# Prompt attention of a hybrid decoder layer: transposing and splitting a head's probabilities one turn ahead of its value products

## The chip, the cores and the metric

The kernel runs on one core of a Trainium2 chip. The metric is the device time of one execution in microseconds. The core's engines run their own instruction queues in order and wait for one another by semaphores: TensorE (PE in the profile; its weight loads are PEld), VectorE (DVE), ScalarE (ACT), GpSimd (POOL) and SyncE (SP), which here only issues DMAs.

## The reference

One layer of a decoder serves 512 prompt tokens and 8 x 4 sample tokens with shared weights: a gated feed-forward, a mixer of four recurrent (HGRN2) and four latent-attention (MLA) heads, an output projection, and a second feed-forward. Each part has norms before and after it. The change lies in the causal softmax attention of the four MLA heads over the 512 prompt tokens:

```python
s = (jnp.einsum('bqhr,bsr->bhqs', ql, c_kv) + jnp.einsum('bqhd,bsd->bhqs', qr, k_rope)).astype(jnp.float32) * scale
s = jnp.where(k_pos[None, None, None, :] <= qp[None, None, :, None], s, -jnp.inf)
p = jax.nn.softmax(s, axis=-1).astype(c_kv.dtype)
return jnp.einsum('bqhs,bsr->bqhr', p, c_kv)
```

The result is projected per head (`w_uv`), concatenated with the recurrent heads and multiplied by `w_out`. The kernel uses the unabsorbed form: per-head keys and values are made first, so that a head's output is its probabilities times its values.

## The kernel before, in words

Nearly all products are made in three passes of a reduced-precision fp32 type: an operand is split into a high part (a cast on ACT, line 170) and a remainder (a subtraction on DVE, line 171), and high x high, high x low and low x high are accumulated in PSUM. Weights arrive by DMA into `wraw` and are split the same way, by a cast on ACT (`wh`, L250) and a subtraction on DVE (`wl`, L251).

The stages in time: first feed-forward (to about 380 us), recurrent heads (to about 575), latent keys and values, then the prompt attention (about 628 to 698 us), into which the output projection of the first 256 tokens (`project(0)`) is woven; after it the decode attention of the sample tokens and the second feed-forward of the first 256 tokens, interleaved; then the rest.

The prompt attention goes through eight turns: four heads for the first 256 tokens (x = 0), then the same heads for the next 256 (x = 1). A turn's work for one head and half is:

- `soft` (L1202 to L1215): per block of 128 query rows (two per turn, qt), the scores on PE into a PSUM bank `s`, then maximum on DVE, exponential on ACT, reciprocal and scaling on DVE. The probabilities are in `pe`. In turns 0 to 3 a block is 128 or 256 keys wide, in turns 4 to 7 384 or 512.
- `value`, which first transposes `pe` on PE in pieces of 128 x 128 into a PSUM bank `tp` (L1225), splits each bank into `PTh` (ACT, L170) and `PTl` (DVE, L171), and then makes the products with the values into a bank `o` (L1234), six of them in turns 0 to 3 and twelve in turns 4 to 7. ACT copies `o` out (L1236).

`soft` runs two turns ahead of `value` (LOOK = 2). Around them stand in each turn: the query projection of a later head (`prep`, L259 with `acc<-q`, turns 0 and 1), the split of a query half (`qsplit_n`), the latent query of the sample tokens (`latent`, L1184 and L1185, turns 0 to 3), and from turn 4 the output projection (`acc<-uha` under L259; its columns are copied by L784 and squared into the norm's sum `ssp` by L298 and L300). The first half of the projection's inputs, the recurrent heads, is there early, so its first column is also begun early. After the last column the sum is made by L191, the norm's factor `s_post` by L197 and L198, and DVE multiplies and adds (L312, L313) to make the inputs `uha` (L207) and `ula` (L208) of the second feed-forward, whose products are L277.

Between these stand small pieces of the decode attention: copies of `qsT` (L1243 on ACT, L1245 on DVE), and the scores of the new tokens (L1317 and L1318 on PE, their maximum L1320 on DVE).

The order on each engine is not the order of the text. A scheduler places the instructions by their place in the text (earlier is more urgent) and by its own estimate of when their inputs are ready. PSUM has eight banks: four for `acc`, and four that `s`, `tp`, `o`, `qa` and `pr` take in a fixed cycle of tags, `CYC = ("ps", "po", "ps", "pm")`, where ps has two banks and po and pm one each. A tile that takes a bank waits until the reader of the tile before it is done. `pe` has three buffers (PEB), `PTh` and `PTl` two (PTB).

Of the kernel before, what the change touches and what calls it, by code (L numbers as in the profile page):

```python
# [110 lines left out]
def hybrid_step_kernel(  # L111
# [18 lines left out]
    def mk(shape, dt, tag, bufs=1, pool=None):  # L130
        return (pool or cur[-1]).tile(shape, dt, name=tag, tag=tag, bufs=bufs)
# [10 lines left out]
    def ps(name, tag="ps", own=False):  # L142
        if tag == "ps" and not own:
            tag = CYC[turns[0] % 4]
            turns[0] += 1
        return pp.tile([P, 512], F32, name=name, tag=tag, bufs=NPS[tag])

    def f32(ap):
        return ap.bitcast(F32)
# [19 lines left out]
    def split(hi, lo, src, eng=None):  # L169
        nc.scalar.copy(hi, src)  # L170
        (eng or nc.vector).tensor_tensor(lo, src, f32(hi), op=ALU.subtract)  # L171
# [121 lines left out]
    def wcols(w, k0, kt, c0):  # L293
        return w[c0 // P, :, k0 : k0 + kt]
# [494 lines left out]
    with scope("mix") as mx_:  # L789
# [5 lines left out]
        q0 = mk([P, 2, KQ, W2], F32R, "q0", pool=dK)  # L795
# [287 lines left out]
        with scope("at2"):  # L1083
# [83 lines left out]
            def prep(hd):  # L1167
                w = weight([w_q[hd]], KQ)
                a = [gemm(w, Q[x]) for x in BOTH]
                qn = mk([P, HS[0]], F32, "qn", QNB)  # L1170
                g = W2 - HS[0]
                nc.vector.tensor_tensor(qn, a[0][:, : HS[0]], s_q[0][:, : HS[0]], op=ALU.mult)
                nc.vector.tensor_tensor(qnb[:, hd, :g], a[0][:, HS[0] :], s_q[0][:, HS[0] :], op=ALU.mult)
                nc.vector.tensor_tensor(qnb[:, hd, g:], a[1], s_q[1], op=ALU.mult)
                qsplit_n(hd, 0, qn)

            def qsplit_n(hd, x, qn):
                qq[hd, x] = [mk([P, 2 * P], F32R, n, 2) for n in ("qnh", "qnl")]
                split(*qq[hd, x], qn[:, : 2 * P])
# [35 lines left out]
                    nc.vector.tensor_scalar_mul(pe[:, :N], pe[:, :N], sm)  # L1215
                return pes

            def value(hd, x, pes):
                q0 = 2 * x
                PTh = mk([P, 4, 2 * P], F32R, "PTh", PTB)  # L1220
                PTl = mk([P, 4, 2 * P], F32R, "PTl", PTB)
                for qt in (q0, q0 + 1):
                    tp = ps("tp")
                    for k in range(qt + 1):
                        nc.tensor.transpose(tp[:, k * P : (k + 1) * P], pes[qt][:, k * P : (k + 1) * P], ident)  # L1225
                    ds = slice((qt - q0) * P, (qt - q0 + 1) * P)
                    split(PTh[:, : qt + 1, ds], PTl[:, : qt + 1, ds], tp.rearrange("p (k t) -> p k t", k=4)[:, : qt + 1])
                o = ps("o")
                n = 0
                hs = slice(hd * P, (hd + 1) * P)  # L1230
                for k in range(q0 + 2):
                    lo = P if k == q0 + 1 else 0
                    for a_, b_ in ((Vh, PTh), (Vh, PTl), (Vl, PTh)):
                        nc.tensor.matmul(o[:, lo : 2 * P], a_[:, k, hs], b_[:, k, lo:], start=n == 0, stop=n == 3 * q0 + 5, skip_group_check=True)  # L1234
                        n += 1
                nc.scalar.copy(oT[x][:, NH + hd, : 2 * P], o[:, : 2 * P])  # L1236
# [21 lines left out]
            heads = [(hd, x) for x in BOTH for hd in range(NH)]  # L1258
            for hd in range(LOOK):
                prep(hd)  # L1260
            pe_ = [soft(*heads[i]) for i in range(LOOK)]
            pj = None
            for i, (hd, x) in enumerate(heads):
                if i + LOOK < len(heads):
                    if i + LOOK < NH:
                        prep(i + LOOK)
                    else:
                        qsplit_n(i + LOOK - NH, 1, qnb[:, i + LOOK - NH])
                    pe_.append(soft(*heads[i + LOOK]))
                if i < NH:  # L1270
                    latent(i)
                if i == PJ0:
                    pj = project(0, to_ffn)
                    next(pj)
                value(hd, x, pe_[i])
                if i == NH - 1:
                    dq = mk([P, 2, KQ * HS[1]], F32, "q1", pool=dK)
                    qbd = [dq[:, 0, k * 320 : (k + 1) * 320].rearrange("p (j q) -> p j q", j=10) for k in range(2)]
                    qrep = dq[:, 1, : 10 * P].rearrange("p (j q) -> p j q", j=10)
                    nc.gpsimd.memset(dq[:, 0, :640], 0.0)  # L1280
                if i == DP:
                    decode_prep()
                    qsplit(0)
                for _ in range(PJ[i]):
                    next(pj, None)
                if i in W1:
                    w0.append(weight([wcols((w_g, w_u)[W1.index(i)][1], 0, KD, 0)], KD))
# [422 lines left out]
```

## Time and profile before

| what | value |
|---|---|
| median of 3 runs | 1250.35 us (1250.27 to 1250.57) |
| the profiled execution, its own time | 1243.16 us |
| its span, first to last instruction | 1241.4 us |
| mean granted TensorE clock | 0.999 |
| PE, DVE, ACT, POOL busy | 98%, 79%, 60%, 6% of the span |
| transposes of the probabilities (L1225) | 40, from 636.5 to 694.5 us |
| casts and subtractions of `tp` into PTh and PTl | 16 and 16, from 636.9 to 696.3 us |

A row of the profile in order of time gives start, duration, engine, line, operation, output and inputs, their shapes and the count of merged instructions; in brackets stands how long the engine was idle before it and what ended the idle time. Durations overlap: products of 256 columns follow each other every 0.12 us though each lasts 0.28. The profiled execution is one execution, 7.19 us faster than the median of the runs, so sums are made against its own time and then carried over as differences.

### The profile page before, as it was taken

What the parts mean: (1) busy time and instruction counts of PE and PEld (TensorE: products, weight loads), DVE (VectorE), ACT (ScalarE), POOL (GpSimd) and SP (SyncE); (2) the same over time, 40 slices, a digit from 0 to 9 for tenths busy, and PEclk for the clock granted to TensorE, in tenths of its full rate; (3) what the DMA queues carried; (4) which work ended last, traced back from release to release, by engine and by line L of the source; (5) the groups of instructions that cost most, each with busy time, mean ns of one, the idle gap of its engine ahead of it and who ended that gap; (6) DMA issues with size and microseconds to landing.
All of it is one profiled execution on the core that took longest, in us unless ns stands there. A gap on an engine that the chain in (4) does not pass through costs nothing.

```text
span 1241.4 us, 29997 instructions
## 1 busy us (share of the span) xinstructions
PE 1215.0 (98%) x12366; PEld 1151.3 (93%) x12366; DVE 982.7 (79%) x1976; ACT 738.8 (60%) x1559; POOL 76.5 (6%) x80
## 2 busy tenths in 40 slices
PE   8999999999999999999999999999999999999997
PEld 6999999999999989988898888888888999999997
DVE  7897788878678888786877899999998778566665
ACT  7675545455366744545758766666656776554455
POOL 0000000000000000000001312322310000000000
PEclk9999999999999999999999999999999999999999
DMA  6232333232264213333233868878776635545451
GB/s 238 86 115 90 103 103 102 86 99 91 62 221 147 82 54 105 88 94 130 85 105 117 339 214 303 310 282 323 258 275 232 198 106 188 184 137 188 150 151 60
DMA packets 73113, 195.59 MB, mean 158 GB/s; under 512 B 12336, under 2 KB 27728, under 8 KB 68240
## 3 DMA queue, kind: packets, MB, share of 16 engines
q1 hardware_dynamic: 64512, 150.47, 37.3%
q0 software_dynamic: 7168, 41.95, 9.2%
q8 instruction: 97, 1.59, 0.5%
q10 hardware_dynamic: 1296, 1.26, 0.3%
q14 instruction: 40, 0.33, 0.1%
HBM read 183.97 MB, written 9.67 MB: 156 GB/s over the span
## 4 chain that ended last, share of the span: by engine, by line
PE 79%; DVE 11%; ACT 7%; issue 2%; DMA 2%; SPq 0%; DVEq 0%; ACTq 0%
PE acc L259 29%; PE acc L277 13%; PE dn L259 8%; PE Y L575 7%; PE X L575 4%; PE Z L575 4%; DVE kh L1381 3%; PE acc L731 3%; DVE wl L251 2%; ACT wh L250 1%; PE s L1393 1%; ACT pbuf L1417 1%; DMA wraw<-w_g 1%; PE pa L952 1%; PE o L1426 1%
## 5 line engine op out<-in xcount | busy, mean ns | idle before, releaser
L250 ACT CAST wh<-wraw 128x1024 fp32r<-128x1024 f32 (+2 forms) x194 | 185.0, 957 | 164.3 <-PE acc L259 103.7
L251 DVE TENSOR_TENSOR wl<-wraw,wh 128x1024 fp32r<-128x1024 f32 (+2 forms) x194 | 214.6, 1108 | 72.2 <-ACT wh L250 71.6
L277 PE MATMUL acc<-uha,wh 128*128 128x256 f32 (+1 forms) x528 | 155.5, 295 | 0.1
L277 PE MATMUL acc<-uha,wl 128*128 128x256 f32 (+1 forms) x528 | 150.0, 285 | 0.8 <-DVE wl L251 0.7
L277 PE MATMUL acc<-ula,wh 128*128 128x256 f32 (+1 forms) x528 | 150.5, 286 | 0.0
L259 PE MATMUL acc<-uhb,wh 128*128 128x288 f32 (+1 forms) x432 | 128.0, 296 | 0.0
L259 PE MATMUL acc<-uhb,wl 128*128 128x288 f32 (+1 forms) x432 | 127.0, 295 | 1.0 <-DVE wl L251 0.8
L259 PE MATMUL acc<-ulb,wh 128*128 128x288 f32 (+1 forms) x432 | 127.5, 295 | 0.0
L277 PEld LDWEIGHTS acc<-uha,wh 128*128 128x128 f32 x528 | 99.2, 188 | 8.8 <-issue 7.9
L277 PEld LDWEIGHTS acc<-uha,wl 128*128 128x128 f32 x528 | 99.2, 188 | 2.3 <-DVE wl L251 1.6
L277 PEld LDWEIGHTS acc<-ula,wh 128*128 128x128 f32 x528 | 99.4, 188 | 1.6 <-issue 1.2
L259 PEld LDWEIGHTS acc<-uhb,wl 128*128 128x128 f32 x432 | 81.2, 188 | 1.6 <-DVE wl L251 1.6
L259 PEld LDWEIGHTS acc<-uhb,wh 128*128 128x128 f32 x432 | 81.0, 187 | 0.2 <-ACT uhb L170 0.2
L259 PEld LDWEIGHTS acc<-ulb,wh 128*128 128x128 f32 x432 | 81.1, 188 | 0.1
L259 PE MATMUL dn<-hh,dh 128*128 128x272 f32 x256 | 74.3, 290 | 0.0
L259 PE MATMUL dn<-hh,dl 128*128 128x272 f32 x256 | 73.7, 288 | 0.0
L259 PE MATMUL dn<-hl,dh 128*128 128x272 f32 x256 | 73.6, 288 | 0.0
L277 PE MATMUL acc<-uhb,wh 128*128 128x272 f32 x176 | 52.8, 300 | 0.0
L1417 ACT COPY pbuf<-pt 32x64 f32<-32x64 f32 x192 | 46.5, 242 | 10.1 <-DVE pt L1413 7.3
L259 PE MATMUL acc<-hlb,wh 128*128 128x288 f32 x176 | 52.1, 298 | 0.0
L259 PE MATMUL acc<-hhb,wh 128*128 128x288 f32 x176 | 51.8, 298 | 0.0
L1393 PE MATMUL s<-kh,q 64*32 64x128 f32 x2560 | 48.0, 273 | 3.5 <-DVE kh L1381 3.5
(632 smaller groups left out, 3881.3 us busy)
## 6 DMA issues: line engine op xcount, KB each, us to landing
wraw<-w_u SPq DMA_DIRECT2D x66, 512.0 KB, 4.3
wraw<-w_g SPq DMA_DIRECT2D x65, 512.0 KB, 3.9
wraw<-w_d SPq DMA_DIRECT2D x40, 384.0 KB, 3.5
wraw<-w_in SPq DMA_DIRECT2D x24, 512.0 KB, 3.5
wraw<-w_d SPq DMA_DIRECT2D x32, 320.0 KB, 3.1
wraw<-w_d SPq DMA_DIRECT2D x16, 512.0 KB, 3.8
wraw<-w_o SPq DMA_DIRECT2D x16, 512.0 KB, 3.7
g_S<-state SPq DMA_DIRECT2D x4, 512.0 KB, 4.4
```

Source lines behind the costliest of these rows:

```text
L250: nc.scalar.copy(wh[:, :kt], w[:, :kt])
L251: nc.vector.tensor_tensor(wl[:, :kt], w[:, :kt], f32(wh[:, :kt]), op=ALU.subtract)
L259: nc.tensor.matmul(out, a, b, start=n == 0, stop=n == last)
L277: nc.tensor.matmul(acc[:, :n], a[:, k], b[:, k], start=k + i == 0, stop=k == kt - 1 and i == 2)
L575: nc.tensor.matmul(bank, a[p][:, k], b[q][:, k], start=first and k + n == 0, stop=k == 3 and n == 2, skip_group_check=True)
L731: nc.tensor.matmul(accs[x, d], wts[d][p][:, k], hs[k // 2][q][:, k % 2, x], start=k + n == 0, stop=k == nf - 1 and n == 2)
L952: nc.tensor.matmul(po[es, c].rearrange("p (n m) -> p n m", m=m), kx[:, cs], up(qx[:, cs], m), start=True, stop=True, skip_group_check=True)
L1381: nc.vector.transpose(kh[:, g].rearrange("p a j k -> p a (j k)"), src)
L1393: nc.tensor.matmul(self.s[r][c * 32 : c * 32 + 32, :P], q[rs, j], kh, start=st + jj == 0, stop=st == len(JS) - 1 and jj == 1, skip_group_c ...
L1417: (nc.scalar.copy if g else nc.vector.tensor_copy)(self.p[g * 32 : g * 32 + 32, c // 2, c % 2 * 4 : c % 2 * 4 + 4, self.i * 16 : self.i * ...
L1426: nc.tensor.matmul(o[g : g + 32, :R], self.p[:, c, a], self.craw[c][:, a], start=i + c == 0 and a < 4, stop=i + c == 2 and a >= 4, skip_gr ...
```

## The change

`value` is cut in two: `lay` transposes and splits, `value` makes the products. `lay` of turn 0 is called ahead of the loop, and in turn i `lay` of turn i + 1 is called ahead of `value` of turn i. No buffer count changes, and no instruction is added or removed.

```diff
-            def value(hd, x, pes):
+            def lay(x, pes):
                 q0 = 2 * x
                 PTh = mk([P, 4, 2 * P], F32R, "PTh", PTB)
                 PTl = mk([P, 4, 2 * P], F32R, "PTl", PTB)
...
                     ds = slice((qt - q0) * P, (qt - q0 + 1) * P)
                     split(PTh[:, : qt + 1, ds], PTl[:, : qt + 1, ds], tp.rearrange("p (k t) -> p k t", k=4)[:, : qt + 1])
+                return PTh, PTl
+
+            def value(hd, x, PTh, PTl):
+                q0 = 2 * x
                 o = ps("o")
                 n = 0
...
             pe_ = [soft(*heads[i]) for i in range(LOOK)]
             pj = None
+            pt_ = [lay(heads[0][1], pe_[0])]
             for i, (hd, x) in enumerate(heads):
...
                     next(pj)
-                value(hd, x, pe_[i])
+                if i + 1 < len(heads):
+                    pt_.append(lay(heads[i + 1][1], pe_[i + 1]))
+                value(hd, x, *pt_[i])
```

In the changed kernel the lines behind `lay` have higher numbers: the products are L1238, the copy of `o` L1240, the copies of `qsT` L1247 and L1249, the maximum of the new tokens' scores L1327.

The scheduler's order changes from the third query projection to the first steps of the decode attention, about 6% of PE's queue; before and behind it, and on SP and POOL throughout, it is the same. Three places follow. The first is PE behind the scores of turn 1 (`s<-causb,idb` is the last of them; `acc<-q` is the third query projection, q_4791 its split input).

```order
 L1204 LDWEIGHTS idb
 L1204 MATMUL s<-causb,idb 128x128
+L1225 MATMUL tp<-ident,pe 128x128
 L259 MATMUL acc<-q_4791,wh 128x272 x2
 L259 MATMUL acc<-q_4791,wl 128x272
+L1225 MATMUL tp<-ident,pe 128x128 x2
 L259 MATMUL acc<-q_4791,wh 128x272 x2
```

Turn 0's three transposes moved to here from behind turn 0's latent query, one projection later; turn 1's now stand there.

The second place is ACT in turns 3 and 4 (`ma<-o` is the copy of turn 3's output, `q<-qsT` the small copies of the decode attention, whose tile has another number in each kernel, the 512-wide exponential turn 5's and the 384-wide one turn 6's).

```order
-L170 CAST PTh<-tp 128x128
-L170 CAST PTh<-tp 128x2x128
-L1243 COPY q_8192<-qsT 32x128 x3
+L1247 COPY q_8207<-qsT 32x128
+L170 CAST PTh<-tp 128x3x128
+L1247 COPY q_8207<-qsT 32x128
+L170 CAST PTh<-tp 128x4x128
 L1213 ACTIVATE pe,sm<-s,mx 128x512
-L1243 COPY q_8192<-qsT 32x128 x6
+L1247 COPY q_8207<-qsT 32x128 x7
+L1240 COPY ma<-o 128x256
 L1213 ACTIVATE pe,sm<-s,mx 128x384
```

Turn 4's casts, 384 and 512 wide, took the place of turn 3's, 128 and 256 wide, and the copy of turn 3's output moved ahead of the 384-wide exponential, behind one small copy more. Further down in that queue the first of two weight casts (L250) moved behind five small copies.

The third place is DVE behind the projection's last column (L312, L313 and L208 make the inputs of the second feed-forward; the first two rows are turn 6's subtractions before, and turn 7's in the changed kernel).

```order
 L171 TENSOR_TENSOR PTl<-tp,PTh 128x3x128
 L171 TENSOR_TENSOR PTl<-tp,PTh 128x4x128
-L171 TENSOR_TENSOR PTl<-tp,PTh 128x3x128
+L1327 TENSOR_REDUCE mx<-s 128x1
+L1329 COPY q_8207<-mx 128x128
 L312 TENSOR_TENSOR ma<-ma,s_post 128x512 x2
-L313 TENSOR_TENSOR q_8227<-q_8227,ma 128x512 x2
-L171 TENSOR_TENSOR PTl<-tp,PTh 128x4x128
-L208 SCALAR_TENSOR_TENSOR ula<-q_8227,gv,uha 128x256 x4
+L313 TENSOR_TENSOR q_8242<-q_8242,ma 128x512 x2
 L312 TENSOR_TENSOR ma<-ma,s_post 128x512 x2
```

Turn 7's two subtractions left this stretch (they are now its first two rows), the maximum of the new tokens' scores moved ahead of the first L312, and the second pair of L312 ahead of the first `ula`.

## The prediction

> **What bounds the kernel now.** I read the profile's page first, then the windows of ten microseconds around the lines of the change, then the waits of TensorE (PE) between 620 and 760 us, and last the rows in order of time at each of those waits.
>
> ```profile
> PE 1215.0 (98%) x12366; PEld 1151.3 (93%) x12366; DVE 982.7 (79%) x1976; ACT 738.8 (60%) x1559; POOL 76.5 (6%) x80
> ```
>
> PE is busy 1215.0 of 1241.4 us, and the change neither adds nor removes an instruction. It can only fill or open gaps in PE's row, and 26.4 us of gap is all there is in the whole program. In a window row the columns are the stretch, its length, then the busy time of PE, PEld, DVE, ACT and POOL, the granted clock, the share of the DMA engines and GB/s.
>
> ```profile
> 650.00:660.00 10.00, 9.05 (x58) 7.08 (x57) 8.48 (x33) 8.53 (x28) 0.00 (x0) 1.00 0.00 0
> 660.00:670.00 10.00, 9.20 (x73) 8.74 (x73) 7.80 (x21) 9.65 (x26) 0.00 (x0) 1.00 0.16 54
> 690.00:700.00 10.00, 7.71 (x55) 6.76 (x56) 9.24 (x17) 8.00 (x20) 3.37 (x3) 1.00 0.62 238
> 700.00:710.00 10.00, 9.87 (x79) 9.44 (x78) 10.00 (x23) 5.59 (x14) 6.13 (x5) 1.00 0.96 354
> ```
>
> The prompt attention runs from about 628 to 698 us. PE's gaps are 0.95, 0.80 and 2.29 us in the first three rows, 4.0 us together. Two other engines are near full in places: ACT with 9.65 of 10 in 660 to 670, DVE with 9.24 and 10.00 from 690 on. The waits that made PE's gaps (engine, line, what it waited for: total, times, longest):
>
> ```profile
> PE o L1234 <- ACT PTh L170: 2.4, 2, 1.7
> PE tp L1225 <- ACT ma L1236: 1.0, 1, 1.0
> PE acc L259 <- DVE wl L251: 0.8, 1, 0.8
> PE tp L1225 <- ACT qsT L1185: 0.3, 1, 0.3
> ```
>
> Only the first row, 2.4 us, is value products waiting for the cast of their own transposes, which is what the change takes out of the way. It is 0.19% of the time. The second and fourth are transposes waiting for a PSUM bank that ACT still reads, the third is a weight of the projection.
>
> **The change part by part.** The 40 transposes (L1225), 16 casts (L170) and 16 subtractions (L171) of all eight heads stay; DMA issues and POOL keep their order. What moves is where they stand in PE's, ACT's and DVE's queues, and, since the scheduler writes the order anew, a few neighbours. I follow three places, called A, B and C, and name each head by its turn, 0 to 7.
>
> *A, turn 0 pulled in front of the third query projection.* Turn 0's transposes now follow directly behind the scores of turn 1. Here are PE's row at that place, DVE's two scalings that make turn 0's probabilities ready, and where the transposes stand before.
>
> ```profile
> 630.24 0.49 PE L259 MATMUL acc<-q,wh 128*128 128x272 f32 x2
> 630.88 0.29 DVE L1215 TENSOR_SCALAR pe<-pe,sm 128x128 f32<-128x128 f32 x1
> 631.47 0.35 DVE L1215 TENSOR_SCALAR pe<-pe,sm 128x256 f32<-128x256 f32 x1
> 636.53 0.31 PE L1225 MATMUL tp<-ident,pe 128*128 128x128 f32 x1
> ```
>
> Before, PE went on with the projection at 630.24 and came to the transposes at 636.53, long after the probabilities were there. Now the first transpose stands at 630.24 and its input is ready at 630.88 + 0.29 = 631.17: PE stops for 0.93 us, and the projection, whose inputs are there (it ran at 630.24), is queued behind it. The second pair needs 631.82; PE gets there at about 631.17 + 0.14 + 3 x 0.13 = 631.7, another 0.1 us. PE was full from 620 to 640 and the next waits of ACT and DVE there are for PE, so the loss is passed on. A = +1.0 us. Bounds: +0.4 if half of it comes back at the wait for qsT at 645.5 us (0.3) and the score wait after it, +1.1 if nothing does.
>
> *B, turns 1 to 5, 644 to 670 us.* The rows are those of the 1.0 us wait, of turn 4's last product, of ACT's two weight casts of the projection, and of PE's wait for the second of these.
>
> ```profile
> 657.27 1.83 ACT L1243 COPY q<-qsT 32x128 f32<-32x128 f32 x6
> 659.70 0.36 ACT L1236 COPY ma<-o 128x256 f32<-128x256 f32 x1
> 660.12 0.66 PE L1225 MATMUL tp<-ident,pe 128*128 128x128 f32 x4 [0.98 <-ACT ma L1236]
> 664.26 0.27 PE L1234 MATMUL o<-PTh,Vl 128*128 128x128 f32 x1
> 662.66 1.05 ACT L250 CAST wh<-wraw 128x1024 fp32r<-128x1024 f32 x1
> 667.85 1.05 ACT L250 CAST wh<-wraw 128x1024 fp32r<-128x1024 f32 x1
> 670.21 0.39 PE L259 MATMUL acc<-uha,wl 128*128 128x256 f32 x1 [0.76 <-DVE wl L251]
> ```
>
> The wait at 660.12 stays in kind: the transposes (now turn 5's) still stand behind turn 3's products, in the same bank, and ACT still runs its small copies (1.83 us, now seven) before it empties the bank. L1236 now stands ahead of the 384-wide exponential, so the wait ends some 0.4 us earlier, at about 659.7. Turn 4's twelve products follow with their casts done and PE is through with them near 661.7 instead of 664.26, with about 1.0 us more work behind it, counted in products. That lead has no taker: the projection's next weights come from ACT. Between 654 and 668 ACT now casts turns 4 and 5 instead of 3 and 4. By form the casts take:
>
> ```profile
> L170 ACT CAST PTh<-tp 128x512 fp32r<-128x512 f32 x4 | 2.4, 588 | 0.1
> L170 ACT CAST PTh<-tp 128x384 fp32r<-128x384 f32 x4 | 1.9, 478 | 0.4 <-PE tp L1225 0.4
> L170 ACT CAST PTh<-tp 128x256 fp32r<-128x256 f32 x4 | 1.5, 372 | 0.4 <-PE tp L1225 0.4
> L170 ACT CAST PTh<-tp 128x128 fp32r<-128x128 f32 x4 | 1.1, 267 | 0.0
> ```
>
> That is 588 + 478 - 372 - 267 = 427 ns more on an engine with 0.35 us to spare in ten, so the cast at 667.85 slides to about 668.3 and PE's restart at 670.21 to 670.6. The first weight (662.66) is also put behind five small copies, 5 x 0.3 = 1.5 us, and becomes a new wait of PE of about 0.8 us, paid out of the 1.0 us lead. B = +0.4 us. Bounds: -1.7 us if both waits (0.98 and 0.76) vanish, +1.0 us if the late first weight delays the second by its own 1.5 us less the 0.5 us that ACT could close up.
>
> *C, turns 6 and 7 at the end of the projection, 688 to 702 us.* Turn 6's transposes are done in turn 5; turn 7's take their place.
>
> ```profile
> 688.94 0.93 PE L1225 MATMUL tp<-ident,pe 128*128 128x128 f32 x7
> 691.57 0.39 PE L1234 MATMUL o<-PTh,Vh 128*128 128x256 f32 x1 [1.70 <-ACT PTh L170]
> 691.32 0.41 DVE L300 TENSOR_TENSOR ssp<-ssp,sq 128x256 f32<-128x256 f32 x1
> 691.88 0.67 PE L191 MATMUL pr<-ssp,ones 128*128 128x256 f32 x2
> 692.96 0.47 ACT L170 CAST PTh<-tp 128x384 fp32r<-128x384 f32 x1
> 693.94 1.28 DVE L312 TENSOR_TENSOR ma<-ma,s_post 128x512 f32<-128x512 f32 x2
> 695.49 0.39 PE L1234 MATMUL o<-PTh,Vh 128*128 128x256 f32 x1 [0.68 <-ACT PTh L170]
> 695.72 0.86 PE L1317 MATMUL s<-kss,qsT 128*128 128x32 f32 x6
> 696.34 0.68 DVE L171 TENSOR_TENSOR PTl<-tp,PTh 128x512 fp32r<-128x512 f32 x1
> 696.95 1.66 DVE L208 SCALAR_TENSOR_TENSOR ula<-q,gv,uha 128x256 fp32r<-128x256 f32 x4
> 698.42 0.33 PE L277 MATMUL acc<-ula,wh 128*128 128x256 f32 x1
> ```
>
> Both waits of 1.70 and 0.68 us go: turn 6's products run from about 689.4 to 690.9, turn 7's casts fall where turn 6's were. What is late next is the norm of the projection. Its sum (L191) needs ssp, which is ready at 691.32 + 0.41 = 691.73 in both kernels, so PE stands again from 690.9 to 691.8 and L191 moves only by 0.1 us. Then ACT is free of a cast (692.96) and has s_post some 0.4 us earlier. But DVE's queue now has the maximum of the new tokens' scores (L1320) ahead of L312, and these scores stand on PE behind L191 and one product of turn 7: 692.45 + 0.2 + 0.86 + 0.1 = 693.6, and with L1320 and L1322 L312 starts at 693.9 to 694.1, as before. Behind it four blocks of L312 now precede the first ula, where two and a PTl did: 694.0 + 6 x 0.6 = 697.6 against 696.95. PE, done with turn 7 at about 694.9, waits for the first ula until 697.6 + 0.4 = 698.0, against 698.42, and the second four ula come 0.6 us earlier, by the PTl that has left (696.34). C = -0.5 us. Bounds: -2.4 us if both waits vanish and no other comes, +0.7 us if PE needs the first ula 0.65 us later as DVE has it.
>
> From about 712 us every queue has its old order, and DVE is full (10.00 in 700 to 710), so a shift is passed on to the end. Sum: +1.0 + 0.4 - 0.5 = +0.9 us on the profiled execution, 1243.16 us (span 1241.4). The median of the runs shown lies 7.19 us above that execution; I add the difference to the median: 1250.35 + 0.9 = 1251.2 us, and call it no change, since a run of this kernel tells about 0.2%, 2.5 us, from nothing.
>
> **The rivals.**
>
> *The end of the projection gets longer and PE's clock falls back (slower).* In place C PE has a gap from 694.9 to 698.0 with two products in it. The start of the program shows what a pause can do:
>
> ```profile
> 5.36 1.12 PE L506 MATMUL pr<-xq,ones 128*32 128x272 f32 x4 [5.36 <-ACT xq L502]
> 7.48 0.43 PE L259 MATMUL acc<-xl,wh 128*128 128x272 f32 x1
> 7.71 0.43 PE L259 MATMUL acc<-xh,wl 128*128 128x272 f32 x1
> 9.62 0.29 PE L259 MATMUL acc<-xh,wh 128*128 128x272 f32 x1
> 9.75 0.33 PE L259 MATMUL acc<-xl,wh 128*128 128x272 f32 x1
> ```
>
> After 5.36 us of nothing, products start every 0.23 us, and from 9.62 every 0.13. Some 4.2 us at the slow step lose 4.2 x 0.10 / 0.23 = 1.8 us. After the gap of 1.70 us at 691.57 nothing of the kind shows, so the point lies between. If it is passed, and DVE's late ula costs its 0.7 us, the sum is 1.0 + 0.4 + 0.7 + 1.8 = 3.9 us: 1254.3 us. The Trainium skill (TensorE: Matmul & The Clock Gate, Part 1: The HAM clock gate) says that about 3.4 us without work halves the clock and as much work restores it; by it my gap is just too short and the sum stays as it is, while 0.5 us more would decide against the change. For it speaks that DVE decides this place; against it that the two products stand in the gap. 0.12.
>
> *The waits vanish and nothing takes their place (faster).* C gives its whole 2.4 us and B its 1.7 us against A's 1.0: 1250.35 - 3.1 = 1247.3 us. For it speaks that DVE loses 1.1 us of subtractions from its full stretch; against it that ssp, the bank and the weight casts are not touched by the change. 0.10.
>
> *The transposes were early enough anyway.* The two waits of the products in the table are those of turns 6 and 7; the turns before them show none, and A's loss, B's lead and C's gain cancel: 1250.4 us, give or take 0.5. 0.30.
>
> **How the numbers follow.** My forecast of 1251.2 us has 0.48. It and the third rival are no change, 0.78; slower by over 0.2% is the first rival and a little of the forecast's upper bound, 0.13; faster 0.09, most of the second rival. The bounds of the three terms add up to -3.7 and +2.8 us, but A is certain and B and C do not both reach their lower ends; with half of each rival's way the range is 1248.3 to 1253.6 us.
>
> **What would show it.** A: a wait of the first transpose for DVE's scaling of about 0.9 us near 630. B: a wait of transposes for L1236 near 660 of about the old length, and L250 rows later against turn 4's products. C: no product waiting for PTh, L1320 directly before L312, and a PE gap of 2 to 3 us before the first ula product. The forecast is wrong if A shows no wait, if L312 starts over 0.5 us earlier after L191 than before, or if products after the gap at C start every 0.23 us.

## The result, and the profile after

The changed kernel takes 1252.57 us (median of 22 runs, 1249.73 to 1254.25), the kernel before beside it 1250.17 us (22 runs). The ratio is 1.0014, with a 95% interval of 1.0007 to 1.002: about 1.75 us slower (0.9 to 2.5). That is no change by the bound of 0.2%, but not zero. It lies 1.4 us above the predicted 1251.2 us and inside the range.

The profiled execution of the changed kernel took 1252.31 us (span 1250.5 us). It can't be set beside the first profile of before as a whole: chips differ by 7 us in this kernel (two of those used run the kernel before in 1250.3 and 1250.6 us, one in 1243.6 us), and that profile took 1243.16 us. Of the 9.15 us between the two profiles some 6.5 arise behind 720 us. So positions below are counted from the first score of turn 0 (627.62 us before, 628.00 us in the changed kernel) and go to 712 us only; times are compared between kernels that ran on one chip.

First the waits of TensorE (PE) in the changed kernel, 620 to 760 us (total, times, longest):

```profile
PE acc L277 <- ACT uha L207: 1.5, 1, 1.5
PE acc L259 <- DVE wl L251: 1.4, 2, 0.8
PE s L1400 <- issue: 1.3, 3, 0.7
PE acc L277 <- DVE ula L208: 0.9, 1, 0.9
PE tp L1225 <- DVE pe L1215: 0.9, 1, 0.9
PE tp L1225 <- ACT ma L1240: 0.7, 1, 0.7
PE pr L191 <- DVE ssp L300: 0.6, 1, 0.6
```

The change did what it says: no product waits for a cast `PTh` any more, and the two waits of 1.70 and 0.68 us are gone. Five new ones stand in their place (1.54, 0.90, 0.88, 0.68 and 0.59 us); the bank's wait and one for a weight were there before. Up to the first ula product PE waited 4.4 us before (1.70 + 0.98 + 0.76 + 0.68 + 0.3 for qsT) and waits 6.4 us now (1.54 + 0.68 + 0.76 + 0.90 + 0.88 + 0.73 + 0.59 + 0.3).

The windows of ten microseconds around the three places:

```profile
650.00:660.00 10.00, 9.90 (x66) 8.04 (x66) 8.42 (x27) 8.16 (x25) 0.00 (x0) 1.00 0.02 8
660.00:670.00 10.00, 8.60 (x68) 7.73 (x68) 8.50 (x30) 9.69 (x28) 0.00 (x0) 1.00 0.04 7
690.00:700.00 10.00, 7.69 (x60) 6.92 (x58) 7.91 (x14) 7.64 (x18) 1.01 (x1) 1.00 0.92 366
700.00:710.00 10.00, 9.29 (x64) 9.25 (x65) 9.07 (x21) 5.86 (x17) 1.35 (x1) 0.83 0.95 336
```

In the last row the granted clock (third number from the end) is 0.83, and was 1.00 in the first profile of before. Cut finer, in the same columns:

```profile
697.00:700.90 3.90, 1.46 (x10) 1.06 (x10) 3.90 (x8) 3.36 (x8) 1.01 (x1) 1.00 0.83 270
700.95:704.30 3.35, 3.35 (x17) 3.35 (x17) 3.35 (x9) 2.24 (x7) 1.35 (x1) 0.50 0.84 339
704.40:710.00 5.60, 5.60 (x48) 5.56 (x48) 4.67 (x11) 2.57 (x8) 0.00 (x0) 1.00 0.96 334
```

For some 3.4 us TensorE has half its clock. The rows in order of time at that place:

```profile
694.52 0.67 PE L191 MATMUL pr<-ssp,ones 128*128 128x256 f32 x2 [0.59 <-DVE ssp L300]
696.20 0.19 DVE L1327 TENSOR_REDUCE mx<-s 128x1 f32<-128x32 f32 x1 [0.76 <-PE s L1325]
696.57 1.29 DVE L312 TENSOR_TENSOR ma<-ma,s_post 128x512 f32<-128x512 f32 x2
697.34 0.44 PE L1340 MATMUL b<-ident,q 128*128 128x128 f32 x2
697.81 1.05 ACT L250 CAST wh<-wraw 128x1024 fp32r<-128x1024 f32 x1
699.31 0.51 PE L277 MATMUL acc<-uha,wh 128*128 128x256 f32 x2 [1.54 <-ACT uha L207]
700.18 1.67 DVE L208 SCALAR_TENSOR_TENSOR ula<-q,gv,uha 128x256 fp32r<-128x256 f32 x4
700.72 0.43 PE L277 MATMUL acc<-ula,wh 128*128 128x256 f32 x1 [0.90 <-DVE ula L208]
700.94 0.41 PE L277 MATMUL acc<-uha,wl 128*128 128x256 f32 x1
701.15 0.41 PE L277 MATMUL acc<-uha,wh 128*128 128x256 f32 x1
...
704.35 0.28 PE L277 MATMUL acc<-ula,wh 128*128 128x256 f32 x1
704.47 0.28 PE L277 MATMUL acc<-uha,wl 128*128 128x256 f32 x1
```

PE is done with turn 7 and the small product behind it (L1340) at 697.78 and has only two products until 700.72. Then products start every 0.215 us, until 704.35, from where they start every 0.12. Between 700.72 and 704.35 there are some 17 of them: 17 x 0.095 = 1.6 us.

The wait at place A, with the two operations of VectorE (DVE) that end it and its sequel:

```profile
631.26 0.29 DVE L1215 TENSOR_SCALAR pe<-pe,sm 128x128 f32<-128x128 f32 x1
631.69 0.30 PE L1225 MATMUL tp<-ident,pe 128*128 128x128 f32 x1 [0.88 <-DVE pe L1215]
631.85 0.35 DVE L1215 TENSOR_SCALAR pe<-pe,sm 128x256 f32<-128x256 f32 x1
```

And the three at place B:

```profile
661.86 0.66 PE L1225 MATMUL tp<-ident,pe 128*128 128x128 f32 x4 [0.73 <-ACT ma L1240]
668.82 0.39 PE L259 MATMUL acc<-uha,wl 128*128 128x256 f32 x1 [0.68 <-DVE wl L251]
672.90 0.39 PE L259 MATMUL acc<-uha,wl 128*128 128x256 f32 x1 [0.76 <-DVE wl L251]
```

### The profile page after: what moved, and what is told of

The parts are those of the page before. It is cut to its first block, busy times and chain, and to the rows that moved or that the text cites. A ratio compares the mean times of both kernels' runs of the same rounds, so it can differ in the third digit from the quotient of the medians.

```text
span 1250.5 us, 29993 instructions
## 1 busy us (share of the span) xinstructions
PE 1221.5 (98%) x12366; PEld 1154.8 (92%) x12366; DVE 983.3 (79%) x1976; ACT 739.8 (59%) x1559; POOL 74.2 (6%) x80
## 4 chain that ended last, share of the span: by engine, by line
PE 86%; DVE 6%; ACT 5%; issue 1%; DMA 1%; DVEq 0%; SPq 0%; ACTq 0%
PE acc L259 30%; PE acc L277 17%; PE dn L259 8%; PE Y L575 7%; PE X L575 4%; PE Z L575 4%; PE s L1400 3%; PE acc L731 3%; PE o L1433 2%; ACT wh L250 1%; DVE wl L251 1%; DVE kh L1388 1%; PE pa L952 1%; PE acc L288 1%; PE zx L840 1%
## 5 line engine op out<-in xcount | busy, mean ns | idle before, releaser
L250 ACT CAST wh<-wraw 128x1024 fp32r<-128x1024 f32 (+2 forms) x194 | 184.9, 957 | 173.7 <-PE acc L259 107.6
L1400 PE MATMUL s<-kh,q 64*32 64x128 f32 x2560 | 52.0, 273 | 5.2 <-issue 3.4
```

The source lines that it names most:

```text
L250: nc.scalar.copy(wh[:, :kt], w[:, :kt])
L1400: nc.tensor.matmul(self.s[r][c * 32 : c * 32 + 32, :P], q[rs, j], kh, start=st + jj == 0, stop=st == len(JS) - 1 and jj == 1, skip_group_c ...
```

## The experiments

The theory to be tested: A and B are real losses that reach the end; at C the gap lets the clock fall, and that, too, reaches the end. The rivals: what is lost on PE is won back at later waits, or VectorE, which is full from 697 to 712 us, sets the pace, so that a slow TensorE costs nothing; or the clock has nothing to do with this gap.

All twelve in one table. The positions are differences of two rows of each profile: from turn 0's first score to the first ula product, to the sum L191 of `ssq` on PE (the next norm, some 80 products later), and to the first `kh` (the decode attention's first step on DVE). The last column is the stretch at half clock. A line "before, beside" gives the kernel before on the chip that ran the kernels below it.

| kernel | median, us | ratio to before beside it (95%) | ula | ssq | kh | half clock from, for |
|---|---|---|---|---|---|---|
| before (first profile) | 1250.17 | | 70.80 | 80.93 | 79.71 | none |
| changed | 1252.57 | 1.0014 (1.0007 to 1.0020) | 72.72 | 84.05 | 81.77 | 700.92, 3.41 |
| before, beside 1 to 4 | 1250.33 | | | | | |
| 1 changed again | 1252.58 | 1.0013 (1.0004 to 1.0022) | 72.72 | 84.13 | 81.82 | 700.44, 3.41 |
| 2 turn 0 not early | 1250.51 | 0.9995 (0.9986 to 1.0005) | 71.55 | 82.89 | 80.62 | 700.30, 3.41 |
| 3 gap filled | 1249.51 | 0.9997 (0.9987 to 1.0007) | 72.71 | 82.81 | 80.76 | none |
| 4 maximum behind | 1251.65 | 1.0005 (0.9996 to 1.0014) | 72.33 | 83.44 | 82.23 | 701.37, 3.41 |
| before, beside 5 to 8 | 1243.63 | | | | | |
| 5 before again | 1243.21, one run | | 71.85 | 81.45 | 80.24 | 691.58, 3.41 |
| 6 turns 6 and 7 only | 1243.84 | 0.9997 (0.9988 to 1.0006) | 71.08 | 83.18 | 80.92 | 697.15, 6.83 |
| 7 the same, filled | 1243.01 | 0.9994 (0.9985 to 1.0003) | 71.10 | 81.20 | 79.14 | none |
| 8 one us later | 1247.42 | 1.0022 (1.0013 to 1.0031) | 73.76 | 84.87 | 82.61 | 701.28, 3.41 |
| before, beside 9 to 12 | 1250.63 | | | | | |
| 9 changed, third time | 1252.01 | 1.0010 (1.0001 to 1.0019) | 72.71 | 84.05 | 81.79 | 701.17, 3.41 |
| 10 turn 0 not early, filled | 1248.82 | 0.9989 (0.9981 to 0.9998) | 71.50 | 81.58 | 79.53 | none |
| 11 as 7, again | 1247.50 | 0.9985 (0.9975 to 0.9996) | 71.10 | 81.19 | 79.14 | none |
| 12 as 11, maximum behind | 1247.31 | 0.9980 (0.9970 to 0.9989) | 70.72 | 80.58 | 79.37 | none |

### 1 and 9: the changed kernel again

No edit.

> The changed kernel once more, without any edit, as the measure for the three kernels that run beside it. Theory (the change costs time, about half of it because the clock falls after the gap at C): median near 1252.5 us, 1.0007 to 1.002 times the kernel before, with the granted clock at 0.83 or so between 700 and 710 us in most executions. Rival (the 1.75 us come from the chips or executions that the first comparison happened to meet): within 0.5 us of the kernel before, ratio interval around 1.0000.

> The changed kernel without an edit, as the measure for the three that run beside it on the same chip (chips were seen to differ by 7 us in the kernel before: 1250.3 and 1243.6 us). Theory: ratio to the kernel before 1.0007 to 1.002, as twice before; the granted clock at half for 3.41 us near 700 us. Rival (the loss belongs to the chip of the first two comparisons): ratio within 0.9995 to 1.0005 if this is the faster chip.

Measured: 1.0013 and 1.0010 times the kernel before. All three comparisons have an interval above 1, and the three profiles agree within 0.1 us in every position of the table. The loss is the kernel's, not a chip's; that the small loss would vanish is refuted.

### 2: turn 0 back in its own turn

```diff
-            pt_ = [lay(heads[0][1], pe_[0])]
+            pt_ = []
...
-                if i + 1 < len(heads):
-                    pt_.append(lay(heads[i + 1][1], pe_[i + 1]))
+                for j in range(len(pt_), min(i + 2, 8)):
+                    pt_.append(lay(heads[j][1], pe_[j]))
```

> Only turn 0 goes back: its transposes and casts are made in turn 0 again, directly ahead of those of turn 1, and the other seven turns stay one turn ahead. On all engines only these pieces move. Theory (term A is a real loss that is handed on to the end): the wait of 0.88 us for DVE's scaling near 631.7 is gone, turn 2's scores start about 1.5 us earlier against the first score than in the changed kernel, and the time falls by 0.9 to 1.5 us. Rival 1 (what A loses is won back at later waits for ACT or DVE, such as 0.73 us at the bank near 661.9): those waits grow by what A gives and the time stays within 0.3 us of the changed kernel. Both theories expect the clock between 700 and 710 us to fall as in the changed kernel, since C is untouched.

Measured: the wait for L1215 is gone, and the ula product stands 72.72 - 71.55 = 1.17 us earlier. The other waits of PE have the lengths of the changed kernel (0.73 at the bank, 0.68 and 0.76 for the weights), so nothing was won back. The median is 2.07 us lower, more than the 0.9 to 1.5 expected, with intervals (0.9986 to 1.0005 against 1.0004 to 1.0022) that just touch. Term A stands; why the time fell by more than the rows is open.

The clock fell here too, but look where. Windows of this kernel in the columns used above:

```profile
699.00:700.25 1.25, 1.25 (x10) 1.25 (x11) 1.25 (x4) 0.63 (x3) 0.00 (x0) 1.00 0.88 316
700.30:703.70 3.40, 3.40 (x19) 3.40 (x18) 3.40 (x10) 2.02 (x5) 2.13 (x1) 0.50 0.88 369
703.80:710.00 6.20, 6.20 (x54) 6.16 (x53) 5.26 (x11) 2.77 (x7) 1.03 (x1) 1.00 0.97 328
```

Its ula product starts at 698.97, and for 1.3 us PE runs without a gap at full clock. Only then, in the midst of full work, the clock is halved.

### 3: the gap filled

```diff
             for i in range(2):
-                nc.tensor.matmul(b_[:, i * P : (i + 1) * P], mxb[:, i], ident, start=True, stop=True)
+                for c in (0,) + (2,) * (8 - 8 * i): nc.tensor.matmul(b_[:, (c or i) * P : ((c or i) + 1) * P], mxb[:, i], ident, start=True, stop=True)
```

> Eight extra products of 128 columns are put on TensorE behind turn 7's last product, into an unused part of a PSUM bank that nobody reads; the rest of all queues is as in the changed kernel. They are extra work and fill 1.0 to 1.7 us of the gap from 697.8 to 700.7, ahead of the wait for uha that lasts 1.54 us; no data that is waited for comes earlier by it. Theory (the gap lets the clock fall, and that costs time at the end): the granted clock stays at 1.00 between 700 and 710 us, products behind the gap start every 0.12 us instead of every 0.215, some 17 of them save 17 x 0.095 = 1.6 us on TensorE, and the time falls by 0.8 to 1.6 us. Rival 1 (VectorE sets the pace from 697 to 712 us, so a slow TensorE costs nothing): the clock stays up, but the time is within 0.3 us of the changed kernel. Rival 2 (the fall is not set by this gap): the products still start every 0.215 us.

Rows of this kernel's TensorE (x18 because each of the nine products of this type counts as two), and a window behind:

```profile
697.27 2.22 PE L1340 MATMUL b<-ident,q 128*128 128x128 f32 x18
699.25 0.50 PE L277 MATMUL acc<-uha,wh 128*128 128x256 f32 x2
700.65 0.39 PE L277 MATMUL acc<-ula,wh 128*128 128x256 f32 x1 [0.90 <-DVE ula L208]
700.88 0.27 PE L277 MATMUL acc<-uha,wl 128*128 128x256 f32 x1
700.99 0.28 PE L277 MATMUL acc<-uha,wh 128*128 128x256 f32 x1
```

```profile
700.65:704.30 3.65, 3.65 (x28) 3.49 (x29) 3.65 (x9) 2.54 (x8) 2.13 (x1) 1.00 0.92 354
```

The uha and ula products start as in the changed kernel (ula at 72.71 us), the clock stays at 1.00, and products start every 0.12 us. The sum L191 of ssq comes 84.05 - 82.81 = 1.24 us earlier. With more work the median is lower: 1249.51 against 1252.58 us, 0.9997 against 1.0013. That is more than the 0.8 to 1.6 us expected, and more than the rows give; why is open. Rival 2 (the fall isn't set by this gap) is refuted. Rival 1 (VectorE hides it) is refuted by the positions up to the first kh, which is 1.01 us earlier. The time alone doesn't decide it: the two intervals overlap a little, and experiment 10, whose interval lies clear of the changed kernel's, undoes A as well.

### 4: the maximum of the new tokens behind L313

```diff
...
-            nc.vector.tensor_tensor(h[x][:, ks], h[x][:, ks], mT[:, ks], op=ALU.add)
+            mix3[x] = nc.vector.tensor_tensor(h[x][:, ks], h[x][:, ks], mT[:, ks], op=ALU.add)
...
-            nc.vector.tensor_reduce(mx, s[:, :TS], axis=AX.X, op=ALU.max)
+            with tc.issue_after(mix3[0].ins): nc.vector.tensor_reduce(mx, s[:, :TS], axis=AX.X, op=ALU.max)
```

> The maximum of the new tokens' scores is held back on VectorE until the last L313, so that L312 no longer stands behind it; the small product that it feeds (L1340) moves behind some 60 products of the second feed-forward. Theory (the maximum ahead of L312 makes the first ula late and the gap long): L312 starts 0.4 us earlier, at the end of s_post, the two operations of the maximum (0.3 us) are out of the way, the first ula product starts about 0.6 to 0.7 us earlier; if the gap is then short enough for the clock the time falls by 1.0 to 2.0 us, if not by 0.3 to 0.7 us. Rival (the end of the projection is set by s_post and the six operations behind it, and the later maximum delays the decode attention as much): within 0.3 us of the changed kernel.

L312 starts 0.39 us earlier, directly behind `s_post`, and the ula product 72.72 - 72.33 = 0.39 us earlier; 0.6 to 0.7 had been expected. In the changed kernel `s_post` is ready at 696.15 us and the scores at 696.17, so the maximum waits no longer than `s_post` does; its two operations, from 696.20 to 696.57, are all that L312 loses. The clock still falls. The first kh comes 0.46 us later. The time, 1.0005, lies between the changed kernel and before, and its interval overlaps both: not settled by the time alone.

### 5: the kernel before again

No edit.

> The kernel before once more, for a second profile: the first one's execution was 7.19 us under the median of its runs, so its part behind 712 us can't be set beside the others. Theory: up to 712 us its rows stand as in the first profile (the granted clock at 1.00 behind the gap at 691.57, the first L191 of ssq some 80.9 us after the first score), and the part behind takes about 5 us longer than in the first. Rival: the rows before 712 us differ too, and then the readings of A, B and C in the first profile were chance.

The theory falls in one point, and it is the most useful one. This execution of the kernel before has the fall as well. Windows, then two rows of its TensorE:

```profile
688.90:690.50 1.60, 0.00 (x0) 0.00 (x0) 1.37 (x2) 1.60 (x6) 1.02 (x2) 1.00 0.96 392
690.60:691.50 0.90, 0.90 (x4) 0.69 (x5) 0.90 (x3) 0.35 (x1) 0.90 (x1) 1.00 1.02 419
691.60:694.90 3.30, 3.30 (x17) 3.12 (x16) 2.48 (x5) 1.64 (x4) 0.00 (x0) 0.50 0.90 344
695.10:700.00 4.90, 4.23 (x35) 4.00 (x34) 4.60 (x10) 4.38 (x10) 1.14 (x1) 1.00 0.07 27
```

```profile
692.47 0.41 PE L1234 MATMUL o<-PTh,Vh 128*128 128x256 f32 x1
692.68 0.41 PE L1234 MATMUL o<-PTl,Vh 128*128 128x256 f32 x1
```

Behind the same gap (1.69 us here, 1.70 in the first profile, where it left no trace) turn 6's products start every 0.21 us. Up to the gap all positions agree with the first profile within 0.03 us. Counted from the first score the first kh is 0.53 us later by it; the execution's time is still the first one's (1243.21 against 1243.16 us), as its first score came 0.94 us earlier and the part behind kh took 0.45 us longer. The part behind 712 us did not take 5 us longer than in the first profile; that difference belongs to the chip.

### 6: only turns 6 and 7 ahead

```diff
-            pt_ = [lay(heads[0][1], pe_[0])]
+            pt_ = []
...
-                if i + 1 < len(heads):
-                    pt_.append(lay(heads[i + 1][1], pe_[i + 1]))
+                for j in range(len(pt_), i + 2 if i in (5, 6) else i + 1):
+                    pt_.append(lay(heads[j][1], pe_[j]))
```

> Only turns 6 and 7 are transposed one turn ahead, turns 0 to 5 as in the kernel before. Against the second experiment (turn 0 alone put back) this undoes B; from 690 us on every queue has the changed kernel's order. Theory (B is a loss of 0.8 to 1.1 us that comes from ACT's work standing ahead of the weight casts): the waits of 0.68 and 0.76 us for the two weights fall back to one of about 0.8, the sum of the projection (L191 of ssp) stands 64.2 to 64.4 us after the first score instead of 65.35, and the time falls by another 0.8 to 1.1 us against the 1250.51 us of that experiment, to about 1249.5 us. Rival 1 (the weights wait for their transfers, not for ACT): the wait stays and the time is within 0.3 us of 1250.5. Both expect the clock to fall to half near 700 us as in the changed kernel, unless the shift of 2.3 us against it matters.

The one weight wait of 0.8 us and the bank's 1.0 us are those of before, so the two weights wait for ACT's order and not for transfers. The ula product is 71.55 - 71.08 = 0.47 us earlier than in experiment 2: this is B. The sum L191 of ssp comes 64.89 us after the first score, against an expected 64.2 to 64.4 and 64.26 before: C alone puts it 0.63 us later. The time doesn't show B: 0.9997 here and 0.9995 in experiment 2, on different chips, with intervals that overlap. In the profiled execution, the slowest of the eleven, the clock fell for 6.83 us, two steps instead of one, and ssq lies 0.29 us behind experiment 2's.

### 7 and 11: the same, filled

The edits of 6 and 3 together.

> The kernel of the sixth experiment with the eight extra products of the third in the gap. It keeps of the change only what C was to give, without the fall of the clock. Theory (A, B and the clock are separate losses that add up): 1.3 us less on TensorE at the L191 of ssq than without the filling, C's own gain is left, and the time is 1.5 to 2.5 us under the kernel before, near 1248.2 us, ratio 0.998 to 0.999. Rival (VectorE's full stretch behind 697 us takes back what C gives): the time equals the kernel before within 0.5 us.

> The kernel of the seventh experiment once more, for a narrower interval and beside the tenth. Theory (what turns 1 to 5 cost is PE's waits and a turn's transposes pulled ahead, and VectorE is 0.57 us ahead of the kernel before at the first kh): 0.4 to 0.7 us under the tenth, 0.4 to 0.7 us under the kernel before, ratio 0.9994 to 0.9997. Rival (the gain at kh is taken back behind it): the kernel before within 0.3 us.

Without the fall of the clock L191 of ssq is 1.98 us earlier than in experiment 6. What is left of the change, C without its clock, has the ula product 0.30 us later than before, but the first kh 0.57 us earlier (79.14 against 79.71), as VectorE has less to do between L312 and kh (told below under C). The times are 0.9994 (interval to 1.0003, not told from 1) on the faster chip and 0.9985 (0.9975 to 0.9996) on a slower one. The theory's 1.5 to 2.5 us was reached on the second chip alone (about 1.9 us by the ratio), where only 0.4 to 0.7 had been expected; why the gain is larger there is open. Against experiment 10 the median is 1.32 us lower, and the intervals overlap.

### 8: the gap one microsecond later

```diff
-    def gemm(wt, act_):
+    def gemm(wt, act_, pre=0):
...
-        n = act_[0].shape[-1]
+        n = act_[0].shape[-1]; [nc.tensor.matmul(acc[:, :n], wh[:, 0], act_[0][:, 0], start=True, stop=False, skip_group_check=True) for _ in range(pre)]
...
-            acc = gemm(weight([wcols(w_o, 0, KD, d * P)], KD), (oh, ol))
+            acc = gemm(weight([wcols(w_o, 0, KD, d * P)], KD), (oh, ol), 9 * (x == 0 and d == 6))
```

> The changed kernel with nine extra products (the first product of the projection's seventh column, repeated and then overwritten) where TensorE is full, so that all of C, the gap with it, comes 1.07 us later against the start of the program; nothing else moves. In four executions so far the clock fell at the same 689.49 us after it first rose, and for 3.41 us, though the gap stood at places that differ by 1.4 us. Theory (the clock is decided on a fixed raster of 3.41 us and the gap is long enough wherever it lies): the fall comes at 689.49 or at 692.90 us after the rise, again for 3.41 us, and the time rises by 1.0 us against the changed kernel. Rival 1 (it depends on how the gap lies in the raster): no fall in this kernel, and the time stays within 0.4 us of the changed kernel or falls. Rival 2 (the fall follows the end of the gap): it comes 1.07 us later than in the changed kernel.

The ula product came 1.04 us later, the clock did not wait for it:

```profile
698.00:701.20 3.20, 1.31 (x10) 0.91 (x8) 3.20 (x6) 2.63 (x6) 1.02 (x1) 1.00 0.52 174
701.30:704.60 3.30, 2.85 (x13) 2.85 (x14) 3.30 (x9) 2.18 (x7) 1.08 (x1) 0.50 0.96 345
704.80:710.00 5.20, 5.20 (x45) 5.15 (x44) 4.49 (x10) 2.68 (x8) 0.44 (x1) 1.00 0.97 339
```

The fall stands at 701.28, before the ula product at 701.75; in the changed kernel 0.20 us behind it, in experiment 2 1.33 us behind it. By the trace's record of the granted clock it is 689.49 us after the clock's first rise, as in the changed kernel. The ratio of 1.0022 is 0.0008 above the changed kernel's, 1.0 us, as the theory had it, though on another chip and with intervals that overlap. Rival 2 (the fall follows the end of the gap) and rival 1 (no fall in this position) are refuted.

### 10: turn 0 back and the gap filled

The edits of 2 and 3 together.

> Turn 0's transposes back in turn 0 (second experiment) and the gap filled (third experiment) together. Theory (the two losses add up): against the first score the L191 of ssq stands at 82.8 - 1.15 = 81.65 us and the first kh at 79.6 us, no fall of the clock, and the time is 1.5 to 2.5 us under the changed kernel beside it, within 0.5 us of the kernel before. Rival (either saving alone already meets the same limit behind 712 us): no faster than the better of the two alone, 0.9995 to 0.9997 times the kernel before or more.

L191 of ssq at 81.58 (expected 81.65) and kh at 79.53 (79.6): the savings add up. In time this kernel takes 0.9989 (0.9981 to 0.9998) of before, the changed kernel beside it 1.0010 (1.0001 to 1.0019). These intervals don't meet: undoing A and filling the gap together are worth about 2.6 us, more than the changed kernel's whole loss.

### 12: filled, with the maximum behind

Experiment 11 with experiment 4's edit, and the filling from the identity:

```diff
+            with tc.issue_after(mix3[9].ins): [nc.tensor.matmul(s[:, P : 2 * P], ident, ident, start=True, stop=True, skip_group_check=True) for _ in range(8)]
```

(`mix3[9]` is the last value product; the eight extra products write where nobody reads.)

> Turns 6 and 7 ahead, the gap filled by eight products of the identity with itself into an unused part of a bank, and the maximum of the new tokens' scores held back until behind the last L313 as in the fourth experiment. Theory (first ula 0.4 us earlier, as the fourth experiment showed, and no fall of the clock): the ula product 70.7 us after the first score against 71.1, L191 of ssq at about 80.8, and 0.3 to 0.6 us less than the eleventh, which would make it the fastest of all. Rival (VectorE's stretch is only turned round: what L312 gains the first kh loses, 0.46 us in the fourth experiment): within 0.3 us of the eleventh or slower.

The waits of its TensorE, 620 to 760 us:

```profile
PE tp L1225 <- ACT ma L1240: 1.0, 1, 1.0
PE s L1401 <- issue: 1.0, 3, 0.4
PE acc L259 <- DVE wl L251: 0.8, 1, 0.8
PE pr L191 <- DVE ssp L300: 0.6, 1, 0.6
PE acc L277 <- DVE ula L208: 0.5, 1, 0.5
```

The ula product at 70.72 and ssq at 80.58 are the earliest of all, and 0.9980 (0.9970 to 0.9989) is the best ratio: 2.5 us under the kernel before by the ratio, and by the medians 4.7 us under the changed one beside it. It beats both. Against experiment 11 the intervals overlap, so that the later maximum helps is not shown by the time; the first kh is 0.23 us later, as the rival said.

## Why the prediction was right, and where it was not

VectorE is the full engine behind 700 us, so the terms are summed at the first kh, from pairs of experiments that differ in one thing:

| term | predicted, us | measured at the first kh, us | from |
|---|---|---|---|
| A | +1.0 | +1.15 (81.77 - 80.62) | changed against 2 |
| B | +0.4 | +0.39 (79.53 - 79.14) | 10 against 11 |
| C, clock kept up | -0.5 | -0.57 (79.14 - 79.71) | 7 and 11 against before |
| sum of these | +0.9 | +0.97 | |
| fall, changed kernel | a rival | +1.01 (81.77 - 80.76) | changed against 3 |
| fall, kernel before | none | +0.53 (80.24 - 79.71) | 5 against the first profile |

By the rows the changed kernel is 1.05 us later where neither kernel has the fall (80.76 - 79.71), 1.53 where both have it (81.77 - 80.24), and 2.06 where it alone has it (81.77 - 79.71). The interval of the time, 0.9 to 2.5 us, holds all three.

How often each kernel has the fall is read from the mean granted clock that is on record for every run. The profiles with a fall have 0.996 or 0.997, those without 0.997 to 0.999, so a run at 0.996 or less is taken to have had one, and a run at 0.998 or more none:

| kernel | runs | mean | 0.998 and more | 0.997 | 0.996 and less |
|---|---|---|---|---|---|
| before, beside the experiments | 96 | 0.9963 | 13 | 35 | 48 |
| changed, in all three comparisons | 44 | 0.9966 | 7 | 21 | 16 |
| filled (3, 7, 10, 11, 12) | 56 | 0.9978 | 41 | 14 | 1 |

The kernel before has falls at least as often as the changed one, and its first profile, at 0.999, was one of the few runs without. So the fall is hardly what sets the two apart in time, though it costs both. Where in the program the falls of a run lie is known only for the profiled ones. Filling one gap all but ends them, so most of those of the changed kernel lie at this place; for the kernel before only experiment 5 shows where.

The forecast's sum was right, and the verdict of no change with it. Most of the loss is A: with turn 0 alone put back, experiment 2 has the mean granted clock of the changed kernel beside it (0.9967 in both) and is back at the time of before (0.9995, 0.9986 to 1.0005). What the forecast had wrong are the way to C, and that behind a gap of 1.70 us the clock stays up.

**A** was right: 0.88 us of wait against 0.93, and nothing of it comes back, as experiment 2 showed. It is a little over its upper bound of 1.1 at the kh and at the ula product (1.17); where what goes beyond the wait arises is not shown.

**B** was right: the waits are 0.73 + 0.68 + 0.76 = 2.17 us against 0.98 + 0.76 = 1.74, a loss of 0.43. The bank's wait shrank by 0.25 us (predicted 0.4), and the first weight became the new wait (0.68, predicted 0.8).

**C** came out right on VectorE by luck, by two errors that nearly cancel. One step was wrong: "its sum (L191) needs ssp, which is ready at 691.32 + 0.41 = 691.73 in both kernels". It isn't. By the end of the projection PE has done one turn's transposes more than before (7 of 0.13 us, 0.93 us in all), so the last column, its copy and ssp come later: L191 by 0.63 us in experiment 6, where A and B are undone. L312 is late by as much, and the ula product comes 0.28 us later than before instead of 0.4 us earlier. What pays for it is larger than I had it: from L312 to the first kh VectorE takes 12.18 us in experiment 7 (694.96 to 707.14) against 13.39 before (693.94 to 707.33). The 512-wide subtraction PTl has left that stretch, 0.61 us, and so has the maximum of the new tokens' scores, which now stands ahead of L312; experiment 4, which puts it behind again, has the first kh 0.46 us later. Rows of before:

```profile
703.19 0.18 DVE L1320 TENSOR_REDUCE mx<-s 128x1 f32<-128x32 f32 x1
707.33 0.70 DVE L1381 STREAM_TRANSPOSE kh<-rraw 128x512 f32<-128x512 f32 x1
```

The rest of C was as told: no product waits for PTh, L1327 stands ahead of L312, and six operations of 0.6 us lead to the first ula (696.57 + 6 x 0.6 = 700.17; the row has 700.18).

**The first rival** was given 0.12 with 1254.3 us. Its mechanism is in all three profiles of the changed kernel, but, as the table of clocks shows, not as something that the change adds. Products behind the gap start every 0.215 us, which the last part of the prediction named as a sign against it. Its price was put at 1.8 us; it is 1.24 us on PE at ssq and 1.01 us on VectorE. What failed is the argument about its condition: "against it that the two products stand in the gap" and "after the gap of 1.70 us at 691.57 nothing of the kind shows, so the point lies between". The two products didn't help, and in experiment 5 that very gap has the fall behind it. One execution had been read as the kernel's rule. The length of the gap alone doesn't decide, as the last section shows.

**The other two rivals** are refuted for the changed kernel: the losses neither cancel nor is it faster.

## What to carry to other kernels

Work that is moved forward delays everything between its new place and its old one, even where it waits for nothing; it pays only if what it delays isn't on the path, so count the moved work at the next thing that waits for the engine's last result. And a gap of 1.7 us can be enough to halve TensorE's clock for the next 3.4 us, in one execution and not in the next: before a difference between two kernels is put down to it, compare the granted clock of many runs of both. If nothing useful can be put into the gap, a few products that nobody reads can be cheaper than the gap: they brought the first kh 1.01 us forward here.

## What the runs showed of the hardware that I had not expected

The clock is decided on a fixed raster. In all eight profiles with a fall, it comes 682.66, 686.08 or 689.49 us after the clock's first rise (which itself stands between 8.9 and 11.9 us) and lasts 3.41 or 6.83 us: 200, 201, 202 and 1 and 2 steps of 3.413 us. How long PE was busy in the step ahead of the fall, by its rows: 0.98 to 1.01 us (the three of the changed kernel), 1.44 (8), 1.51 (4), 1.72 (5), 1.83 (2), 2.11 (6). In the six profiles without a fall the least busy step at this place has 2.5 us or more, except the first profile of before, with 1.72. So no empty step is needed. But busy time doesn't draw the line: the kernel before has 1.72 us both with a fall and without, and experiment 6, whose clock fell behind a step with 2.11, has a later step with 1.84 (a wait of 1.40 us in it) and no fall:

```profile
693.74:697.15 3.41, 2.11 (x17) 1.88 (x16) 2.83 (x7) 2.00 (x5) 1.02 (x1) 1.00 0.51 195
751.77:755.18 3.41, 1.84 (x64) 1.17 (x66) 3.34 (x10) 2.60 (x12) 0.00 (x0) 1.00 0.86 324
```

What does draw it is open. The work in the step at half clock seems to count too: behind 2.56 us of it (experiment 6) the clock stayed down for a second step, behind 2.94 (8) and 3.41 (the others) it came back.

The Trainium skill (TensorE: Matmul & The Clock Gate, Part 1: The HAM clock gate) describes a free-running window of 3413 ns; the raster in these traces agrees. The page lets the clock fall after an idle window and warns of gaps over some 3.4 us; the traces differ: here waits of 1.54 and 0.90 us, with 0.98 us of work in the step, were enough.

Still open: two of the chips need more time between 720 and 945 us, at a granted clock of 1.00; for one kernel (experiment 11 against 7) it is 4.4 us. No experiment was made on it.
